# A mixture-of-experts layer in which the block for an expert's slots past 64 is split into an up half and a down half, with the ordinary up products between them

## The chip, the cores and the metric

The kernel runs on one core of a Trainium2 chip. The metric is device microseconds (us) of one execution; lower is better. Engines are named as the profile names them: PE is TensorE (PEld its weight loads), DVE is VectorE, ACT is ScalarE, POOL is GpSimd, SP is SyncE, which issues every DMA here. A name with a q behind it (PEldq, SPq) means the engine's sequencer.

## What is computed

One residual layer on 256 tokens of width 1024: a mixer (differential attention beside a gated linear recurrence), a layer norm, a top-4-of-32 mixture of experts with a clamped SwiGLU, and a second layer norm. The change lies in the mixture of experts alone:

```python
logits = xt @ w_router + b_router
top_v, top_e = lax.top_k(logits, 4);  gates = softmax(top_v)
# for each expert e and the tokens that chose it:
h = xb @ w_gu[e] + b_gu[e]                    # 1024 -> 2048, bias b_gu
x_glu = minimum(h[..., ::2], 7.0);  x_lin = clip(h[..., 1::2], -7.0, 7.0)
y = (x_glu * sigmoid(1.702 * x_glu) * (x_lin + 1.0)) @ w_down[e] + b_down[e]
out[token] += gate * y
```

All arithmetic is float32. The weights of the 32 experts are 403 MB, each read once.

## The kernel before

The first 125 us or so hold the mixer, the first norm and the router. The rest is a loop over the experts. Every expert has 64 fixed slots (CAP): a matmul with a one-hot matrix gathers its tokens' activations, 64 columns per expert. Tokens past the 64th of an expert go to overflow blocks of 32 slots (OCAP), which run under a branch on the expert's token count.

**Weights.** `load_chunk` loads an expert's weights in six chunks of 2 MB, four for the up product (w_gu, one DMA each) and two for the down product (w_down, two DMAs of 1 MB each), into ten slots that are used in turn. `ahead` issues, on SP's queue and in this order, the load that goes into a slot when the matmuls that read the slot have been issued; the DMA itself waits for those matmuls. At most eight DMAs are under way: the issue of one also waits for the landing of the one eight before it.

**One ordinary expert on PE** (PE and SP run in the order written; DVE, ACT and POOL are ordered by a planner within each stretch between branches):

1. `overflow(e)`: the branch L1011 on the count; in most cases its body is jumped over.
2. `first(e)`: 64 matmul passes of up products (`gu_mm`, L892). The bias is already in the accumulators (`begin_gu`, L679, fp32r). While these run, `ready(e + 1)` (L1002) loads the count of the next expert into registers of PE, DVE and ACT, and gives PE a prefetch hint for the branch. DVE and ACT do the SwiGLU (L902 to L906).
3. `finish`: the combine of the pair of experts before (L954, with adds on DVE, L956). Odd experts: the transposes of the gates (`gate_t`, L948, copied by ACT, L950).
4. `act_t`: transposes of the activations (L913), each followed by the next expert's bias (`begin_gu`).
5. `need`: the gather of a later pair's columns (L797), then the down products (L925), and the next expert.

The pool `mc` has three PSUM tiles that the combines, transposes, gathers and overflow blocks use in turn, so that a stage that takes a tile waits until the stage three tiles before has been read out.

**The overflow block before** (`more`), at the head of the expert's iteration: gather of 32 columns, bias (four f32 matmuls, L688), up products in four groups of 32 columns (L892), SwiGLU, transposes of activations and gates (L913, L981), down products (L988), copy (L991), eight small combines with eight adds on DVE (L996, L997). In this input one expert has more than 64 tokens, and no more than 96: the block runs once. It is expert 25, since six more experts follow it. Experts 30 and 31 share the last stretch, in which both up products come before the two down products.

## Time and profile before

| | |
|---|---|
| median of 3 runs | 1098.63 us (1097.76 to 1101.21) |
| profiled execution | 1100.57 us, of which the span of the trace is 1098.9 us |
| PE busy | 1008.3 us, 92% of the span |
| mean granted clock of PE | 0.979 of full speed |
| DMA | 423.4 MB, 385 GB/s over the span |

The profiled execution is one execution; 1.7 us of its time lie outside the span. Starts are in us from the span's start.

### The profile page before, as it was taken

How to read it: one execution, taken by the hardware profiler on the slowest of the kernel's cores; microseconds unless marked ns; L12 is line 12 of the kernel's file. 1: busy time of each engine (PE TensorE's matmuls, PEld its weight loads, DVE VectorE, ACT ScalarE, POOL GpSimd, SP SyncE). 2: the span in 40 equal slices, each digit the busy share in tenths (PEclk: the TensorE clock that was granted, in tenths of full speed). 3: DMA queues.
4: the chain of work that ended last, by engine and by line, in shares of the span. 5: the costliest groups of instructions: out<-in, count | busy, mean ns of one | idle time of the engine just before them, and what ended most of it. 6: DMA issues, size and time to landing. Idle time of an engine off the chain costs nothing. (4 is left out here: it accounts for less than half of the span.)

```text
span 1098.9 us, 12603 instructions
## 1 busy us (share of the span) xinstructions
PE 1008.3 (92%) x4948; PEld 472.8 (43%) x4948; DVE 277.8 (25%) x625; ACT 188.7 (17%) x426; POOL 146.6 (13%) x221
## 2 busy tenths in 40 slices
PE   8999999999999889888999989888888989999995
PEld 8987644443444333333334433333323434444431
DVE  6978411121212121213212121212101222121223
ACT  5576211111111111110011111110100101111111
POOL 4583202010101010101001010101001001010101
PEclk8999999999999999999899999999999989999998
DMA  7967799999999999999999999999999949999972
GB/s 268 334 247 318 293 377 426 422 423 423 423 423 423 422 423 423 422 425 426 423 424 420 410 423 412 420 410 394 415 395 411 423 198 424 425 425 422 424 292 82
DMA packets 47193, 423.44 MB, mean 385 GB/s; under 512 B 6365, under 2 KB 6430, under 8 KB 14400
## 3 DMA queue, kind: packets, MB, share of 16 engines
q1 hardware_dynamic: 47040, 421.59, 92.9%
q8 instruction: 73, 1.20, 0.5%
q14 instruction: 80, 0.66, 0.2%
HBM read 420.52 MB, written 1.05 MB: 384 GB/s over the span
## 5 line engine op out<-in xcount | busy, mean ns | idle before, releaser
L892 PE MATMUL h<-we,xg 128*64 128x512 f32 (+1 forms) x2112 | 469.8, 603 | 63.1 <-DMA we<-in_w_gu_dram 50.6
L892 PEld LDWEIGHTS h<-we,xg 128*64 128x64 f32 (+1 forms) x2112 | 161.9, 137 | 368.3 <-issue 295.1
L925 PE MATMUL y<-we,actT 128*64 128x512 f32 x1024 | 228.9, 599 | 0.1
L902 DVE TENSOR_SCALAR g<-h 128x256 f32<-128x256 f32 x65 | 27.6, 425 | 688.3 <-PE h L892 688.3
L940 POOL TENSOR_SCALAR sgate<-iota,posm,gate 128x64 f32<-128x64 f32 x96 | 54.1, 582 | 814.2 <-PE gt_ps L948 813.2
L925 PEld LDWEIGHTS y<-we,actT 128*64 128x64 f32 x1024 | 71.3, 137 | 135.1 <-issue 127.7
L903 ACT ACTIVATE sg<-g 128x256 f32<-128x256 f32 x65 | 27.0, 416 | 589.2 <-DVE g L902 589.2
L797 PE MATMUL xg_ps<-S,n 128*128 128x128 f32 (+1 forms) x544 | 70.5, 284 | 0.0
L797 PEld LDWEIGHTS xg_ps<-S,n 128*128 128x128 f32 x544 | 69.5, 199 | 2.5 <-issue 1.6
L954 PE MATMUL cb<-ysb,gtT 128*128 128x512 f32 x116 | 57.5, 618 | 0.0
L1117 ACT ACTIVATE ysb<-y 128x512 f32<-128x512 f32 x30 | 16.3, 594 | 140.7 <-PE y L925 140.7
L956 DVE TENSOR_TENSOR acc<-acc,cb 128x512 f32<-128x512 f32 x58 | 39.5, 680 | 0.0
L805 DVE TENSOR_SCALAR xg<-xg_ps,gb 128x128 f32<-128x128 f32 (+1 forms) x68 | 22.8, 398 | 61.8 <-PE xg_ps L797 61.8
L389 PE MATMUL pj<-xh,hi 128*128 128x256 f32 x128 | 37.3, 292 | 0.0
L389 PE MATMUL pj<-xh,lo 128*128 128x256 f32 x128 | 36.8, 288 | 0.0
L389 PE MATMUL pj<-xo,hi 128*128 128x256 f32 x128 | 36.8, 288 | 0.0
L913 PE MATMUL actT_ps<-ident,g 128*128 128x128 f32 x130 | 29.9, 312 | 7.3 <-DVE g L906 6.3
L954 PEld LDWEIGHTS cb<-ysb,gtT 128*128 128x128 f32 x116 | 19.6, 189 | 37.4 <-ACT sg L903 23.5
L252 POOL TENSOR_TENSOR lo<-win,hi 128x1024 fp32r<-128x1024 f32 x11 | 32.9, 3014 | 12.3 <-PE pj L389 12.2
L913 PEld LDWEIGHTS actT_ps<-ident,g 128*128 128x128 f32 x130 | 21.6, 202 | 24.8 <-DVE g L906 12.2
L807 ACT ACTIVATE xg<-xg_ps,gb 128x128 f32<-128x128 f32 (+1 forms) x68 | 25.4, 452 | 33.2 <-PE xg_ps L797 33.2
L679 PE MATMUL h<-bgu,pick 128*128 128x512 f32 x64 | 30.5, 479 | 0.0
(271 smaller groups left out, 702.5 us busy)
## 6 DMA issues: line engine op xcount, KB each, us to landing
we<-in_w_gu_dram SPq DMA_DIRECT2D x128, 2048.0 KB, 15.3
we<-in_w_down_dram SPq DMA_DIRECT2D x127, 1024.0 KB, 30.4
win<-in_w_in_dram SPq DMA_DIRECT2D x8, 1024.0 KB, 9.8
wout<-in_w_out_dram SPq DMA_DIRECT2D x4, 1024.0 KB
win<-in_w_in_dram SPq DMA_DIRECT2D x4, 512.0 KB, 8.2
x<-in_x_dram SPq DMA_DIRECT2D x4, 256.0 KB, 3.1
we<-in_w_down_dram SPq DMA_DIRECT2D x2, 512.0 KB
out_dram<-acc SPq DMA_DIRECT2D x4, 256.0 KB, 2.3
```

What stands on the lines that cost most here:

```text
L252: return (eng or V).tensor_sub(lo, src, f32(hi))
L389: PE.matmul(ps[m // 2][:, m % 2], a, b, start=k == 0 and m % 2 == 0 and i == 0, stop=k == KT - 1 and i == 2, skip_group_check=True)
L679: PE.matmul(ps[b], picks[e].rearrange("p g w -> p (g w)"), bgs[b], start=True, stop=False, skip_group_check=True)
L797: PE.matmul(ps[:, (k % 4) * n:(k % 4 + 1) * n], pairs(n1[t])[:, k // 2, k % 2], S[:, t], start=start, stop=t == NT - 1, skip_group_check=True)
L892: PE.matmul(ps[b][g * w:(g + 1) * w], xg[k // 4][:, k % 4, o:o + w], W[e, k][:, c0:c0 + 512], start=False, stop=k == KT - 1, skip_group_ch ...
L902: V.tensor_scalar(g[:, ns], ps[b][:, 0::2], 7.0, None, op0=OP.min)
L903: A.activation(s, g[:, ns], AF.Sigmoid, scale=1.702)
L913: PE.transpose(ps[:, j * P:(j + 1) * P], gj[:, j], ident)
L925: PE.matmul(ps[n][gs], at[:, 2 * b + j, g * CAP:(g + 1) * CAP], w_dn(e, 2 * g + b, j, n * 512, 512), start=c + j == 0, stop=c + j == 4, sk ...
L940: G.tensor_scalar(sg[:, t, i * CAP:(i + 1) * CAP], iota2[:, 0], posm[:, t, o:o + 1], gate[:, t, o:o + 1], op0=OP.is_equal, op1=OP.mult)
L954: PE.matmul(pp, gt[:, n, t * P:(t + 1) * P], y, start=True, stop=True)
L956: V.tensor_add(acc[t][:, ns], acc[t][:, ns], pp)
```

## The change

`more` becomes `more_up` (gather, bias, up products, gate transposes, SwiGLU) and `more_down` (activation transposes, down products, combines). For all experts but the last, `overflow(e)` runs `more_up` at the old place, ahead of the ordinary up products, and `overflow_down(e)` runs `more_down` under a second branch on the same count, behind `finish` and the gate transposes. The rarer blocks past 96 slots are now ahead of the first one within the branch. The load of the next expert's count and its hint (`ready(e + 1)`) move behind the second branch; their old place is taken by a hint for the second branch. The bias of the overflow block is made by two fp32r matmuls over all 128 columns, as that of the ordinary block, with a stationary matrix that DVE spreads out first. The gate matrix is built once and copied three times instead of built four times, and the eight combines go into four PSUM tiles, two to a tile.

```diff
     def begin_more(e):
         ps = mc(f"h{e}")
-        for q in range(4):
-            g, b = q // 2, q % 2
-            pick = two[:, 32 * g + e:32 * g + e + 1].to_broadcast([P, OCAP])
-            PE.matmul(ps[q * OCAP:(q + 1) * OCAP], pick, f32(bgs[b]), start=True, stop=False, skip_group_check=True)
+        pick = wk.tile([P, 2, P], F32R, tag="l", name=f"picko{e}")
+        V.memset(f32(pick), 0.0)
+        for b in range(2):
+            V.tensor_copy(pick[:, b].rearrange("p (g b c) -> p b g c", g=2, b=2)[:, b], picks[e][:, :, :OCAP])
+        for b in range(2):
+            PE.matmul(ps, pick[:, b], bgs[b], start=b == 0, stop=False, skip_group_check=True)
         return {0: ps}
...
-    def more(e, i):
+    def more_up(e, i):
         pm = shifted(e, i)
         xg = gather([e], OCAP, pm, V, "o")
+        sg = wk.tile([P, NT, P], F32, tag="sg", name=f"sgateo{e}")
         for half in range(2):
             gather_mm(*xg, half)
...
+        h = gu_mm(e, xg[1], 0, OCAP)
         for t in range(NT):
-            for g in range(ng):
-                V.tensor_scalar(sg[:, t, g * OCAP:(g + 1) * OCAP], iota2[:, 0, 0:OCAP], pm[:, t, 0:1],
-                                gate[:, t, e:e + 1], op0=OP.is_equal, op1=OP.mult)
+            V.tensor_scalar(sg[:, t, :OCAP], iota2[:, 0, 0:OCAP], pm[:, t, 0:1], gate[:, t, e:e + 1],
+                            op0=OP.is_equal, op1=OP.mult)
+            V.tensor_copy(sg[:, t, OCAP:].rearrange("p (g c) -> p g c", c=OCAP),
+                          sg[:, t, None, :OCAP].to_broadcast([P, P // OCAP - 1, OCAP]))
         ps = mc(f"gto_ps{e}")
         for t in range(NT):
             PE.transpose(ps[:, t * P:(t + 1) * P], sg[:, t], ident)
+        gt = wk.tile([P, T], F32, tag="gto", bufs=1, name=f"gtTo{e}")
         A.activation(gt, ps[:, :T], AF.Copy)
+        g = wk.tile([P, 256], F32, tag="go", bufs=1, name=f"go{e}")
+        swiglu(e, h, 0, g)
+        return g, gt
+
+    def more_down(e, g, gt):
+        ng, n = P // OCAP, 256
+        ao = wk.tile([P, 2, P], F32, tag="l", name=f"actTo{e}")
+        act_t(e, g, 0, ao)
         ps = mc(f"yo{e}")
...
-        for t in range(NT):
-            for g in range(ng):
...
+        for g in range(ng):
+            gs, ns = slice(g * OCAP, (g + 1) * OCAP), slice(g * n, (g + 1) * n)
+            pp = mc(f"cbo{e}_{g}").rearrange("p (t n) -> p t n", t=NT)
+            for t in range(NT):
+                PE.matmul(pp[:, t], gt[gs, t * P:(t + 1) * P], y[gs, :], start=True, stop=True, skip_group_check=True)
+            for t in range(NT):
+                V.tensor_add(acc[t][:, ns], acc[t][:, ns], pp[:, t])
+
+    def more(e, i):
+        more_down(e, *more_up(e, i))
...
+    def overflow_down(e):
+        with tc.If(counts[e] > CAP, preferred_fallthrough_block=True, label=f"down{e}"):
+            more_down(e, *held.pop(e))
...
     for e in range(NE - 1):
         if e > 0:
             overflow(e)
-        g = first(e, lambda i: (i == 3 and ready(e + 1), e == 0 and i == 6 and need(0, V, 1)))
+        g = first(e, lambda i: (i == 3 and hint(f"down{e}", counts[e] > CAP), e == 0 and i == 6 and need(0, V, 1)))
         finish(e % 2)
         if e % 2 == 0:
             sg = gate_rows(e)
         else:
             gt = gate_t(e, sg)
+        overflow_down(e)
+        ready(e + 1)
         at = wk.tile([P, 4, P], F32, tag="actT", bufs=1, name=f"actT{e}")
```

## Rows read from the trace of the kernel before

**Rows 1.** From the page: the span, and the DMA rate in 40 slices of 27.5 us.

```profile
span 1098.9 us, 12603 instructions
...
GB/s 268 334 247 318 293 377 426 422 423 423 423 423 423 422 423 423 422 425 426 423 424 420 410 423 412 420 410 394 415 395 411 423 198 424 425 425 422 424 292 82
```

**Rows 2.** Waits, all of the run, and PE's longest in total from 896 us on: who waited for whom, us in total, times, longest.

```profile
PE h L892 <- DMA we<-in_w_gu_dram: 50.6, 39, 2.4
```

```profile
PE h L892 <- PEq L1011: 0.9, 5, 0.2
```

**Rows 3.** Timeline of PE: the start of the ordinary up products of experts 22, 23, 26 and 29 (start, us, engine, line, operation, out<-in, shape, count, idle before and what ended it).

```profile
773.68 1.90 PE L892 MATMUL h<-we,xg 128*64 128x512 f32 x7 [0.19 <-PEq L1011]
...
804.67 3.65 PE L892 MATMUL h<-we,xg 128*64 128x512 f32 x16 [1.21 <-DMA we<-in_w_gu_dram]
...
925.07 2.37 PE L892 MATMUL h<-we,xg 128*64 128x512 f32 x10 [0.18 <-PEq L1011]
...
1003.65 13.95 PE L892 MATMUL h<-we,xg 128*64 128x512 f32 x64 [0.16 <-PEq L1011]
1017.53 1.98 PE L954 MATMUL cb<-ysb,gtT 128*128 128x512 f32 x4
```

**Rows 4.** Timeline of PE through expert 25: its overflow block, its ordinary up products, combine and gate transposes; and two rows of DVE and ACT in the same stretch.

```profile
869.71 1.94 PE L688 MATMUL h<-bgu,two 128*32 128x512 f32 x8
871.42 6.03 PE L892 MATMUL h<-we,xg 128*32 128x512 f32 x48
879.85 3.50 PE L892 MATMUL h<-we,xg 128*32 128x512 f32 x16 [2.40 <-DMA we<-in_w_gu_dram]
...
886.54 0.70 PE L913 MATMUL actT_ps<-ident,g 128*128 128x128 f32 x2 [3.19 <-DVE g L906]
887.03 0.63 PE L981 MATMUL gto_ps<-ident,sgateo 128*128 128x128 f32 x2
887.71 4.71 PE L988 MATMUL yo<-we,actTo 128*32 128x256 f32 x64
...
892.94 0.71 PE L996 MATMUL cbo<-yo,gtTo 32*128 32x256 f32 x6 [0.51 <-ACTq L1017]
893.67 3.17 DVE L997 TENSOR_TENSOR acc<-acc,cbo 128x256 f32<-128x256 f32 x8 [7.19 <-PE cbo L996]
...
896.83 15.58 PE L892 MATMUL h<-we,xg 128*64 128x512 f32 x64 [0.45 <-PEq L1017]
...
912.33 1.98 PE L954 MATMUL cb<-ysb,gtT 128*128 128x512 f32 x4
...
914.15 0.60 PE L948 MATMUL gt_ps<-ident,sgate 128*128 128x128 f32 x4
...
914.59 0.40 PE L913 MATMUL actT_ps<-ident,g 128*128 128x128 f32 x2
...
914.79 0.60 ACT L950 ACTIVATE gtT<-gt_ps 128x512 f32<-128x512 f32 x1 [1.40 <-PE gt_ps L948]
...
915.83 2.04 PE L797 MATMUL xg_ps<-S,n 128*128 128x128 f32 x16
```

**Rows 5.** Windows of 5 us: busy time of PE, PEld, DVE, ACT and POOL (with instructions), granted PE clock, DMA share, GB/s.

```profile
885.00:890.00 5.00, 3.42 (x28) 1.87 (x32) 1.48 (x6) 0.77 (x2) 0.00 (x0) 0.66 0.65 274
890.00:895.00 5.00, 3.99 (x59) 2.16 (x48) 1.21 (x4) 0.38 (x1) 0.00 (x0) 1.00 0.07 28
895.00:900.00 5.00, 4.55 (x15) 1.68 (x15) 1.72 (x5) 0.00 (x0) 0.00 (x0) 0.67 0.08 29
```

**Rows 6.** The branch and the count on PE's sequencer: line, engine, operation, count; min/median/max ns, first and last start. The first row is of the whole run, the second of 900 to 1030 us, the last two of 896 to 898 us.

```profile
L1011 PEldq COMPARE_BRANCH  x32: 82/783/4019, 125.5 to 1071.0; - x32
```

```profile
L1011 PEldq COMPARE_BRANCH  x5: 359/397/1197, 920.4 to 1025.6; - x5
```

```profile
L1002 PEldq TENSOR_LOAD <-cnt x1: 307/307/307, 896.9 to 896.9; - x1
```

```profile
L1219 PEldq BRANCH_PREFETCH_HINT  x1: 40/40/40, 897.7 to 897.7; - x1
```

**Rows 7.** The end. PE's up products of expert 31 and the down products that come last; what the SP queue waited for in 1050 to 1052 us; and two windows of 5 us (columns as in rows 5).

```profile
1047.34 8.80 PE L892 MATMUL h<-we,xg 128*64 128x512 f32 x40
...
1077.05 7.09 PE L925 MATMUL y<-we,actT 128*64 128x512 f32 x32
```

```profile
SPq L199 <- DMA we<-in_w_gu_dram: 4.6, 1, 4.6
```

```profile
1050.84 0.33 SPq L199 DMA_DIRECT2D we<-in_w_down_dram  x1
```

```profile
1065.00:1070.00 5.00, 4.53 (x21) 1.95 (x19) 0.42 (x1) 0.77 (x2) 0.00 (x0) 1.00 0.07 25
1070.00:1075.00 5.00, 5.00 (x18) 1.49 (x20) 0.00 (x0) 0.00 (x0) 0.00 (x0) 1.00 0.08 26
```

**Rows 8.** From the page: the DMA queues that carry instructions (packets, MB, share of 16 engines). From the timeline of PE: the activation transposes of expert 0.

```profile
q8 instruction: 73, 1.20, 0.5%
q14 instruction: 80, 0.66, 0.2%
```

```profile
144.30 0.50 PE L913 MATMUL actT_ps<-ident,g 128*128 128x128 f32 x2 [1.06 <-DVE g L906]
...
146.10 0.70 PE L913 MATMUL actT_ps<-ident,g 128*128 128x128 f32 x2 [1.07 <-DVE g L906]
```

More of the change, by code (lines that the diff above doesn't have):

```diff
@@ L981, in more @@
             PE.transpose(ps[:, t * P:(t + 1) * P], sg[:, t], ident)
-        gt = wk.tile([P, T], F32, tag="sg", name=f"gtTo{e}")
+        gt = wk.tile([P, T], F32, tag="gto", bufs=1, name=f"gtTo{e}")
         A.activation(gt, ps[:, :T], AF.Copy)
+        g = wk.tile([P, 256], F32, tag="go", bufs=1, name=f"go{e}")
[5 more added lines that the diff above has]
+        act_t(e, g, 0, ao)
         ps = mc(f"yo{e}")
@@ L991, in more @@
         A.activation(y, ps[:, :n], AF.Copy)
-        for t in range(NT):
-            for g in range(ng):
-                gs, ns = slice(g * OCAP, (g + 1) * OCAP), slice(g * n, (g + 1) * n)
-                pp = mc(f"cbo{e}_{t}_{g}")
-                PE.matmul(pp[:, :n], gt[gs, t * P:(t + 1) * P], y[gs, :], start=True, stop=True)
-                V.tensor_add(acc[t][:, ns], acc[t][:, ns], pp[:, :n])
+        for g in range(ng):
[7 more added lines that the diff above has]
+        more_down(e, *more_up(e, i))
     counts = {}
@@ L1008, in overflow @@
     def overflow(e):
-        c = counts.pop(e)
+        c = counts[e]
+        last = e == NE - 1
         with tc.If(c > CAP, preferred_fallthrough_block=True, label=f"over{e}"):
             hint(f"more{e}_1", c > CAP + OCAP)
-            if e == NE - 1:
+            if last:
                 for t in range(NT):
                     V.memset(acc[t], 0.0)
-            more(e, 0)
             with tc.If(c > CAP + OCAP, preferred_fallthrough_block=True, label=f"more{e}_1"):
@@ L1023, in overflow @@
                         more(e, i)
-            if e == NE - 1:
+            if last:
+                more(e, 0)
                 for t in range(NT):
                     fin(t, ident, acc[t])
+            else:
+                held[e] = more_up(e, 0)
+    held = {}
+    def overflow_down(e):
+        with tc.If(counts[e] > CAP, preferred_fallthrough_block=True, label=f"down{e}"):
+            more_down(e, *held.pop(e))
     where = {e: (i, j) for i, g in enumerate(GROUPS) for j, e in enumerate(g)}
```

6 lines of the change are left out of this document (removed).

## Prediction, made before the changed kernel was run

> **What bounds the kernel now.** I read the page's DMA rate first: from slice 7 on, but for the last two, it stands near 420 GB/s, with one hole, 198 GB/s in slice 33, where expert 25's overflow block lies [rows 1]. So the loop streams weights at a nearly constant rate, and PE is close behind. Which of the two sets the pace is read from PE's waits and from the distance of two experts. Ahead of 896 us PE waits for weights 39 times, 50.6 us in all; behind it the longest entry of its waits is a branch, 0.9 us, and there is none for weights [rows 2]. Experts 22 and 23 start 31.0 us apart; from expert 26 to 29 three experts take 78.6 us, 26.2 us each [rows 3]. The reader is to see two stretches: up to expert 25 the weights are the bound, with 4 to 5 us of slack on PE in every expert; the overflow block then puts PE behind by its whole length, the weights run ahead, and from there to the end PE is the bound.
>
> How far ahead are the weights at the end? A DMA issue waits for the landing of the one eight before. The issue at 1050.84 us had waited 4.6 us for a w_gu load [rows 7]; it is the seventh w_down issue behind the eight w_gu loads of experts 30 and 31, so what landed there is expert 31's third chunk. PE uses it from about 1054.2 us: it starts at 1047.34 and makes 16 passes per chunk, 64 of them in 13.88 us [rows 3, 7], so 1047.34 + 32 x 0.217 = 1054.3. The slack is 3.4 us. Nothing that makes PE faster ahead of this can gain more than 3.4 us, unless the weights land sooner.
>
> Would they? In the hole the rate is not zero but 28 GB/s, and again 25 and 26 GB/s in the last stretch, when all other loads are through [rows 5, 7]. That is 1/16 of 424 GB/s: one of the 16 DMA engines is behind the others and still works while they have nothing. A load has landed when its last part has. So the hole is time in which 15 engines wait for slots and the one that decides goes on. I take it that the last landings stay where they are.
>
> **The change, part by part.** All times are in the profiled execution.
>
> *Bias in fp32r.* The eight f32 passes take about 1.7 us up to the first up product (869.71 to 871.42) [rows 4]; two passes of 128 columns may take half of that. The last 16 up products of the block wait for a weight chunk for 2.40 us [rows 4]. What is saved ahead of 879.85 us makes that wait longer: nothing gained. By the same cover the pick matrix that DVE now builds costs nothing, and so does the branch to the rarer blocks, now at the head: DVE's and PE's time there lies inside the wait. Without that cover the bias would be worth 0.8 us.
>
> *The overflow block's stall.* From the end of its up products (879.85 + 3.50 = 883.35) to the ordinary ones (896.83) PE spends 13.5 us: 3.19 waiting for SwiGLU, transposes, 4.71 of down products, 0.51 for a copy, combines held up by DVE's adds, 0.45 for the branch [rows 4]. Afterwards only the two gate transposes remain there, 0.6 us; SwiGLU runs under the ordinary up products. Removed: 12.9 us.
>
> *The same work, now behind the gate transposes.* Added there: 0.4 for the transposes, 0.6 for ACT's copy of the ordinary gates that is ahead of theirs, and 0.3, an estimate, for what their own copy takes beyond that; then the down products, 3.8 us at full clock (4.71 with the first half at 0.66 [rows 4, 5]); 0.5 for the copy; 0.7 to the first add; eight adds in 3.17 us, because the next gather needs the last of the three PSUM tiles back [rows 4]. That is 9.5 us. Under the adds run the ordinary transposes and biases, 1.24 us (914.59 to 915.83 [rows 4]). Added: 8.3 us. Bounds: 6.5 if the combines and adds overlap better, 11 if every copy and add is waited for.
>
> *The clock.* The ordinary up products of expert 25 took 15.50 us (896.83 to 912.33) against 13.88 for expert 29: the granted clock was 0.67 in 895 to 900, after a stretch of waits [rows 3 to 5]. They now follow 16 passes without a pause, so I take the full rate, a gain of 1.6 us. But the thinly filled stretch has only moved, and the low clock may follow it there. I give back half, 0.8 us (bounds 0 and 1.6).
>
> Sum for expert 25: 12.9 - 8.3 + 1.6 - 0.8 = 5.4 us gained, between 1.9 and 8.0.
>
> *A second branch and a moved count, for every expert.* The load of the count and the hint take PE's sequencer 0.86 us (896.88 to 897.74 [rows 6]). At the old place the sequencer is ahead of PE by many passes, and the rows show no wait for it. The new place is behind the second branch. When a body is jumped over, PE first runs dry: in the rows the next work follows a branch with a gap of 0.16 to 0.19 us [rows 3]. Then the 0.86 us follow with PE empty. Less what PE waits for there anyway (the transposes need DVE's SwiGLU), some 0.3 us, I take 0.95 us per expert. Bounds: 0.2 if the sequencer is early enough for all of it, 1.7 if part of a slow branch shows. What is queued behind on PE is the transposes, the gather and the down products; ACT's and DVE's own branch and count lie under these.
>
> Up to expert 25 this is covered by the 4 to 5 us of slack. For the first experts, where SP still waits for PE, PE waits over 1 us for DVE at this very place (expert 0, twice [rows 8]), so the loads do not start later. From expert 26 to 30 there is no cover: 5 x 0.95 = 4.8 us lost, between 1.0 and 8.5.
>
> One rule speaks against this part. The rows: a jump took PE's sequencer 0.08 us at least, 0.78 at the median, 4.02 at most [rows 6], and was mostly hidden, because PE had passes left. The Trainium skill, page "Runtime: NRT & Kernel Launch", section "Instruction fetch mechanics", says that a taken branch whose target is outside the window already fetched stops until a DMA has brought the page. The longest rows agree; by the rule alone every new jump would be exposed, and the five experts would lose far more than 4.8 us. That is the first rival below.
>
> **The sum.** -5.4 + 4.8 = -0.6 us: 1098.3 for the span of 1098.9, 1099.9 for the profiled execution of 1100.57. That execution is 1.9 us above the median; for the median, 1098.63 - 0.6 = **1098.0 us**. What a measurement of this kernel can tell from no change is about 0.3%, 3.3 us.
>
> **The rivals.**
>
> *The new jump stalls PE (slower).* Each of the five late experts pays the time of a slow jump less what PE has queued. For it: jumps of up to 4.02 us [rows 6], with less work queued ahead of the new branch than ahead of the old. Against: most are short, and the hint is given some 14 us ahead. It decides from (5.4 + 3.3) / 5 = 1.75 us per expert; at 3 us it gives 1098.6 - 5.4 + 15 = 1108 us. Chance 0.12.
>
> *More code to fetch delays the weights (slower).* Instructions come by DMA too, 1.86 MB in 153 packets [rows 8], beside the engine that decides the landings. If every added branch puts 1 us in front of it, 25 experts with the weights as bound are 25 us later: about 1120 us. Against: the code is hardly longer, and a jump over a short body lands in what is fetched anyway. Chance 0.06.
>
> *The weights do land sooner (faster).* The hole is about 13 us long at full rate (27.5 us at 198 instead of 424 GB/s lose 14.6 us). The ordinary up products now free their slots some 13 us earlier. If the slots decide and not the one slow engine, the end can move by what PE gains, and PE would have to gain it: 8.0 at most for expert 25, less 1.0: 1098.6 - 7 = 1091.6 us. Against: the 25 to 28 GB/s. Chance 0.14.
>
> *The change does what I say*: 0.68. Its own range: gains end at the 3.4 us of slack, 1095.2; losses at -1.9 + 8.5, 1105.2.
>
> **How the numbers follow.** I predict 1098.0, the likeliest case. The range leaves out the second rival (0.06) and about as much again at each end of the first and the third: 1094.5 to 1107. Within 0.3% ends at 1095.3 and 1101.9. Of the 0.68, 0.58 lies inside, 0.08 above, 0.02 below. Faster: 0.02 + 0.14 = 0.16; slower: 0.08 + 0.12 + 0.06 = 0.26; same: 0.58.
>
> **What would show it.** In expert 25: no wait for DVE behind the last overflow up product, and ordinary up products of 13.9 us that begin near 884; the next expert's begin near 919.7 instead of 925.07. No hole in the rate below 300 GB/s for more than a few us. Experts 26 to 29 at 27 us each instead of 26.2, with a gap on PE ahead of the activation transposes. The last down products start within 3.4 us of 1077.05. I am wrong if the distance of experts 22 and 23 changes, since then the change reaches the stream of weights; if the late experts stay at 26.2 us; or if weights land at the end well ahead of 1075.

## The result and the profile after

The changed kernel is slower: 1112.64 us (median of four, 1110.47 to 1115.91) against 1099.77 us for the kernel before on the same chip; the ratio is 1.0123, interval 1.0103 to 1.0142. I had predicted 1098.0 us, and 1107 us as the upper end. In the profiled executions the span goes from 1098.9 to 1109.2 us, 10.3 us against 12.9 between the medians; the profiled execution of the changed kernel is 1.7 us under its median, that of the kernel before 0.8 us over it. What follows places the 10.3 us.

The page of the changed kernel, span, DMA rate in 40 slices and the two queues that carry instructions (compare [rows 1, 8]):

```profile
span 1109.2 us, 12977 instructions
...
GB/s 258 302 286 326 281 390 427 419 423 423 421 422 421 423 424 422 422 422 424 367 424 420 424 421 421 424 419 420 405 420 410 422 339 346 421 422 423 420 113 77
...
q8 instruction: 109, 1.79, 0.7%
q14 instruction: 86, 0.70, 0.2%
```

The hole of 198 GB/s has become two shallow ones, 339 and 346. Queue 8 went from 73 to 109 packets of 16 KB. It carries PE's code: the section on the hints shows PE's stalls ending just behind its packets.

The timeline of PE through expert 25 (compare [rows 4]):

```profile
870.72 4.46 PE L799 MATMUL xg_ps<-S,n 128*128 128x32 f32 x28 [2.85 <-DVE S L786]
875.99 1.06 PE L799 MATMUL xg_ps<-S,n 128*128 128x32 f32 x4 [0.81 <-issue]
876.86 1.20 PE L690 MATMUL h<-bgu,picko 128*128 128x512 f32 x2
877.99 7.86 PE L894 MATMUL h<-we,xg 128*32 128x512 f32 x64
885.79 0.44 PE L980 MATMUL gto_ps<-ident,sgateo 128*128 128x128 f32 x2
886.15 13.96 PE L894 MATMUL h<-we,xg 128*64 128x512 f32 x64
900.04 1.98 PE L956 MATMUL cb<-ysb,gtT 128*128 128x512 f32 x4
...
912.65 2.55 PE L799 MATMUL xg_ps<-S,n 128*128 128x128 f32 x16
...
922.40 1.08 PE L894 MATMUL h<-we,xg 128*64 128x512 f32 x4 [0.18 <-PEq L1024]
```

The stall between the two groups of up products is gone, and the ordinary ones run at the full rate. But the block starts late: its gather waits 2.85 us for DVE's selection rows (S) and 0.81 us for nothing that the profile names ("issue"), and there is no wait for weights left to hide that.

PE in expert 28, from the same timeline:

```profile
991.34 1.98 PE L956 MATMUL cb<-ysb,gtT 128*128 128x512 f32 x4
994.68 0.48 PE L915 MATMUL actT_ps<-ident,g 128*128 128x128 f32 x2 [1.36 <-DVEq L1046]
...
995.69 0.39 PE L799 MATMUL xg_ps<-S,n 128*128 128x128 f32 x2
1000.05 3.15 PE L799 MATMUL xg_ps<-S,n 128*128 128x128 f32 x14 [3.97 <-issue]
1003.12 8.46 PE L927 MATMUL y<-we,actT 128*64 128x512 f32 x32
```

Two new things: 1.36 us ahead of the activation transposes, which end with something of DVE's sequencer on L1046, the second branch; and a stall of 3.97 us in the middle of the gather, behind which gather and down products run 2.7 us longer than in other experts, since the granted clock was 0.50, its lower level, from 1000 to 1005 us, behind the stall. PE's waits over the whole run have both (us, times, longest):

```profile
PE actT_ps L915 <- DVEq L1046: 22.9, 17, 2.0
PE xg_ps L799 <- issue: 16.4, 5, 4.5
PE actT_ps L915 <- ACTq L1046: 16.0, 13, 1.4
...
PE y L927 <- issue: 6.7, 4, 3.0
```

**Where the time went.** Expert 24 starts at 836.9 instead of 836.0: +0.9. From there to expert 26 (922.40; before 925.07): 85.5 us instead of 89.1, -3.6. From expert 26 to 30 (1039.5): 117.1 us instead of 105.2, +11.9; three of the four intervals are 27.3, 27.8 and 27.7 us where 26.0 and 26.6 were usual, and the one with the stall 34.3. Behind that +1.1, one more gap of 1.19 us. Sum: 0.9 - 3.6 + 11.9 + 1.1 = 10.3 us, the difference of the spans.

### The profile page after: what moved, and what is told of

It is laid out like the page before. It is cut to its first block, busy times and chain, and to the rows that moved or that the text cites. A ratio compares the mean times of both kernels' runs of the same rounds, so it can differ in the third digit from the quotient of the medians.

```text
span 1109.2 us, 12977 instructions
## 1 busy us (share of the span) xinstructions
PE 1008.7 (91%) x4942; PEld 488.4 (44%) x4942; DVE 277.5 (25%) x624; ACT 194.6 (18%) x427; POOL 146.2 (13%) x221
## 5 line engine op out<-in xcount | busy, mean ns | idle before, releaser
L894 PE MATMUL h<-we,xg 128*64 128x512 f32 (+1 forms) x2112 | 457.3, 595 | 14.2 <-DMA we<-in_w_gu_dram 8.8
L894 PEld LDWEIGHTS h<-we,xg 128*64 128x64 f32 (+1 forms) x2112 | 170.7, 136 | 297.6 <-issue 277.9
L927 PE MATMUL y<-we,actT 128*64 128x512 f32 x1024 | 235.2, 609 | 6.8 <-issue 6.7
L904 DVE TENSOR_SCALAR g<-h 128x256 f32<-128x256 f32 x64 | 27.1, 424 | 665.2 <-PE h L894 665.2
L905 ACT ACTIVATE sg<-g 128x256 f32<-128x256 f32 x64 | 26.6, 416 | 514.0 <-DVE g L904 514.0
L799 PE MATMUL xg_ps<-S,n 128*128 128x128 f32 (+1 forms) x544 | 77.7, 300 | 19.2 <-issue 16.4
L799 PEld LDWEIGHTS xg_ps<-S,n 128*128 128x128 f32 x544 | 76.6, 215 | 22.8 <-issue 21.7
L389 PE MATMUL pj<-xo,hi 128*128 128x256 f32 x128 | 36.7, 286 | 0.0
L389 PE MATMUL pj<-xh,lo 128*128 128x256 f32 x128 | 36.7, 286 | 0.0
L916 ACT ACTIVATE actT<-actT_ps 128x256 f32<-128x256 f32 x64 | 24.5, 384 | 68.5 <-PE actT_ps L915 66.3
```

What stands on the lines that cost most here:

```text
L389: PE.matmul(ps[m // 2][:, m % 2], a, b, start=k == 0 and m % 2 == 0 and i == 0, stop=k == KT - 1 and i == 2, skip_group_check=True)
L799: PE.matmul(ps[:, (k % 4) * n:(k % 4 + 1) * n], pairs(n1[t])[:, k // 2, k % 2], S[:, t], start=start, stop=t == NT - 1, skip_group_check=True)
L894: PE.matmul(ps[b][g * w:(g + 1) * w], xg[k // 4][:, k % 4, o:o + w], W[e, k][:, c0:c0 + 512], start=False, stop=k == KT - 1, skip_group_ch ...
L904: V.tensor_scalar(g[:, ns], ps[b][:, 0::2], 7.0, None, op0=OP.min)
L905: A.activation(s, g[:, ns], AF.Sigmoid, scale=1.702)
L927: PE.matmul(ps[n][gs], at[:, 2 * b + j, g * CAP:(g + 1) * CAP], w_dn(e, 2 * g + b, j, n * 512, 512), start=c + j == 0, stop=c + j == 4, sk ...
```

## The experiments

Differences are between medians, kernel less the kernel before on the same chip; the changed kernel itself stands at +12.9. Runs of one kernel spread over some 5 us (one_branch: 1095.2 to 1101.0), so a profile's intervals tell where time goes, and the medians how much.

| kernel | median us | less before | ratio, interval |
|---|---|---|---|
| one_branch | 1098.29 | -0.7 | 1.0001, 0.9990 to 1.0012 |
| count_late | 1099.19 | +0.2 | 1.0008, 0.9996 to 1.0019 |
| count_back | 1107.51 | +8.5 | 1.0081, 1.0067 to 1.0094 |
| spare_branch | 1108.89 | +9.9 | 1.0089, 1.0076 to 1.0103 |
| branch_later | 1105.98 | +6.9 | 1.0060, 1.0045 to 1.0074 |
| spare_one_tile | 1108.39 | +9.3 | 1.0094, 1.0080 to 1.0109 |
| rare_last | 1099.53 | +0.5 | 1.0006, 0.9997 to 1.0014 |
| later_rare_last | 1100.30 | +1.2 | 1.0011, 0.9996 to 1.0027 |
| after_rare_last | 1106.72 | +7.9 | 1.0061, 1.0036 to 1.0085 |
| one_rare_last | 1099.07 | +0.2 | 0.9993, 0.9982 to 1.0004 |
| hint_mid | 1124.93 | +26.1 | 1.0234, 1.0208 to 1.0261 |
| later_hint_mid | 1135.57 | +36.7 | 1.0328, 1.0306 to 1.0350 |
| after_no_hint | 1102.04 | +2.7 | 1.0030, 1.0019 to 1.0042 |
| rare_last_no_hint | 1103.82 | +4.5 | 1.0049, 1.0036 to 1.0062 |
| rare_last_late_no_hint | 1106.02 | +7.0 | 1.0067, 1.0053 to 1.0081 |
| own_tiles | 1098.98 | -0.4 | 0.9997, 0.9986 to 1.0008 |
| own_tiles_no_hint | 1097.59 | -1.8 | 0.9987, 0.9978 to 0.9997 |
| bias_only | 1102.41 | +3.4 | 1.0032, 1.0020 to 1.0044 |

### Is it the second branch?

**one_branch**

```diff
-                held[e] = more_up(e, 0)
+                more_down(e, *more_up(e, 0))
-        g = first(e, lambda i: (i == 3 and hint(f"down{e}", counts[e] > CAP), e == 0 and i == 6 and need(0, V, 1)))
+        g = first(e, lambda i: (i == 3 and ready(e + 1), e == 0 and i == 6 and need(0, V, 1)))
-        overflow_down(e)
-        ready(e + 1)
```

> The changed kernel with one branch again: the block's down products stand right behind its up products, ahead of the ordinary ones, and the count is loaded at its old place, in the middle of the ordinary up products; the fp32r bias, the rarer blocks at the head, the gate transposes ahead of SwiGLU and the four-tile combines stay. Theory S (the second branch on PE's sequencer, with the late count, costs the time): the gap ahead of the activation transposes goes from 1.2-1.4 us back to what DVE's SwiGLU leaves, experts 26 to 30 are 26.2 us apart, the whole run is 12 us or more under the changed kernel, between 1096 and 1101 us. Rival B (the cost is in the block of expert 25 itself, its order, its adds or the slow jump at its head): at most 3 us better than the changed kernel, above 1108 us.

Measured: no difference from the kernel before. All that the change costs is gone with the second branch, its hint and the count that moved with it: theory S, as far as these three go together. What it gains is gone too by the median; in the profile, the fastest of its eleven runs, expert 24 to 26 still take 85.9 us instead of 89.1.

**count_back**

```diff
-        g = first(e, lambda i: (i == 3 and hint(f"down{e}", counts[e] > CAP), e == 0 and i == 6 and need(0, V, 1)))
+        g = first(e, lambda i: (i == 3 and (hint(f"down{e}", counts[e] > CAP), ready(e + 1)), e == 0 and i == 6 and need(0, V, 1)))
         overflow_down(e)
-        ready(e + 1)
```

> The changed kernel with only the load of the next expert's count and its hint back in the middle of the ordinary up products; both branches stay. Theory S1 (most of the loss per expert is the 0.86 us of load and hint behind the drained engine): the gap ahead of the activation transposes falls from 1.2-1.4 to 0.3-0.5 us, experts 26 to 30 gain 0.9 us each, 1108 us; the stalls of 1 to 4.5 us behind the jump stay. Rival S2 (the jump itself and the code behind it are the cost): less than 1.5 us better than the changed kernel.

**count_late** (the kernel before)

```diff
-        g = first(e, lambda i: (i == 3 and ready(e + 1), e == 0 and i == 6 and need(0, V, 1)))
+        g = first(e, lambda i: (e == 0 and i == 6 and need(0, V, 1)))
             gt = gate_t(e, sg)
+        ready(e + 1)
```

> The kernel before with only the load of the count and its hint moved behind the gate transposes; no second branch. Theory S1: 0.86 us per late expert less what DVE is waited for there, 5 x 0.5 to 5 x 0.86, 2.5 to 4.3 us slower than before. Rival S2 (without a branch ahead of it the sequencer runs ahead and hides the load): within 1 us of before.

**spare_branch** (the kernel before; its body never runs)

```diff
+    def spare_down(e):
+        with tc.If(held[e] > CAP + 3 * OCAP, preferred_fallthrough_block=True, label=f"down{e}"):
+            more_down(e, *(f32(bgs[i])[:, :256] for i in range(2)))
-        g = first(e, lambda i: (i == 3 and ready(e + 1), e == 0 and i == 6 and need(0, V, 1)))
+        g = first(e, lambda i: (i == 3 and (hint(f"down{e}", held[e] > CAP + 3 * OCAP), ready(e + 1)), e == 0 and i == 6 and need(0, V, 1)))
             gt = gate_t(e, sg)
+        spare_down(e)
```

> The kernel before with an added branch behind the gate transposes, hinted in the middle of the ordinary up products as in the changed kernel, around the same down part, on a condition that no expert meets; expert 25's block and the count stay as before. Theory S2 (the jump and the code behind it): a gap of 0.3-0.5 us ahead of the activation transposes in every expert, stalls of 1 to 4.5 us behind some of the jumps, one of them among experts 26 to 30: 5 to 9 us slower than before. Theory S1: 1.5 to 2.5 us slower. Rival B: within 1 us of before.

Measured: the late count by itself costs nothing (+0.2), since without a branch ahead of it the sequencer is early. The branch and its hint, without the late count, cost 9.9 us, the size of S2 and more, but not by its mechanism: there is no stall in the gather or the down products. Its late experts are 27.2 and 27.3 us apart instead of 26.0 and 26.6, 1.0 us more on average, or 5 us for five. The other 5 I can only place: expert 24 already starts at 840.9 instead of 836.0. Of these 4.9 us, 1.8 are there when expert 0 starts, ahead of any branch (128.9 us; the kernels lie between 125.0 and 128.9 there); why the rest comes is open. In count_back the same 27.2 and 27.3 stand: the late count is worth 0.3 to 0.5 us of the gap, not the 0.9 of S1, and yet count_back is 4.3 us better than the changed kernel. What it saved is eight of the nine stalls that the profile calls "issue", shown below to be waits for code. The ninth grew to 3.7 us; it lies in expert 25's own gather, and behind it the granted clock was 0.50 (875 to 885 us), so that expert 24 to 26 take 91.6 us here.

### What the branch itself costs

PE's waits in 925 to 1040 us in count_back:

```profile
PE actT_ps L915 <- DVEq L1046: 2.1, 2, 1.1
PE actT_ps L915 <- ACTq L1046: 1.5, 2, 0.7
```

What PE waits for on DVE's and ACT's sequencers is seen in one expert of count_back, in the rows of L1046 (line, engine, operation, count; ns, first and last start):

```profile
L1046 DVEq COMPARE_BRANCH  x1: 56/56/56, 970.4 to 970.4; - x1
L1046 ACTq COMPARE_BRANCH  x1: 45/45/45, 970.8 to 970.8; - x1
L1046 PEldq EVENT_SEMAPHORE  x1: 51/51/51, 970.8 to 970.8; - x1
L1046 DVEq EVENT_SEMAPHORE  x1: 21/21/21, 971.2 to 971.2; - x1
L1046 ACTq EVENT_SEMAPHORE  x1: 17/17/17, 971.4 to 971.4; - x1
```

and in the timelines of DVE, ACT and PE there:

```profile
970.50 0.68 DVE L958 TENSOR_TENSOR acc<-acc,cb 128x512 f32<-128x512 f32 x1
```

```profile
970.78 0.60 ACT L952 ACTIVATE gtT<-gt_ps 128x512 f32<-128x512 f32 x1 [1.41 <-PE gt_ps L950]
```

```profile
971.47 0.50 PE L915 MATMUL actT_ps<-ident,g 128*128 128x128 f32 x2 [0.73 <-ACTq L1046]
```

On DVE and ACT the jump takes 45 to 56 ns. But behind it each engine raises its semaphore by what the skipped body would have added, and does so only when its own work ahead of the branch is done: DVE behind the add that ends at 971.18, ACT behind the gate copy that ends at 971.38. PE starts at 971.47. Before, PE needed neither. In expert 29 its transposes start at 1019.79, while DVE's last add runs to 1020.38:

```profile
1019.79 0.40 PE L913 MATMUL actT_ps<-ident,g 128*128 128x128 f32 x2
```

```profile
1019.70 0.68 DVE L956 TENSOR_TENSOR acc<-acc,cb 128x512 f32<-128x512 f32 x1
```

It needs them now because six tiles of the body and the transposes' tile come in turn from the same three PSUM buffers; the buffer's last reader is, by the program, in the body. Three kernels take this theory (J) apart from the rival that the expectations from here on call S, the jump and the drain of PE's own sequencer.

**branch_later** (count_back)

```diff
-        overflow_down(e)
         at = wk.tile([P, 4, P], F32, tag="actT", bufs=1, name=f"actT{e}")
...
         need(where[e][0] + 1, G, where[e][1])
+        overflow_down(e)
```

> The kernel of count_back (changed kernel, count loaded in the middle of the up products) with the second branch moved on by one step: behind the activation transposes and the gather, ahead of the ordinary down products, which write no tile of the pool that the branch's body uses. Theory J (join: past the jump each engine adds to its semaphore what the body would have added, DVE and ACT only behind all they have queued ahead, and PE's next tile of the shared PSUM pool waits for these additions): the gap of 0.7 and 1.2 us goes, 0.2-0.3 us for the drained engine stays, experts 26 to 30 are 26.2-26.9 apart instead of 27.2-27.3, 3 to 4 us better than count_back: 1103.5 to 1104.5. Rival S (the jump and the drain of PE's own sequencer): the gap of about 1 us only moves to the down products, within 1.5 us of count_back's 1107.5.

**spare_one_tile** (spare_branch, the body's `mc` tiles all one tile)

```diff
-        act_t(e, g, 0, ao)
         ps = mc(f"yo{e}")
+        for j in range(2):
+            PE.transpose(ps[:, j * P:(j + 1) * P], gj[:, j], ident)
...
-            pp = mc(f"cbo{e}_{g}").rearrange("p (t n) -> p t n", t=NT)
+            pp = ps.rearrange("p (t n) -> p t n", t=NT)
```

> The kernel of spare_branch (before, with a branch that no expert takes behind the gate transposes) with a body of the same instructions that uses one tile of the shared PSUM pool instead of six, so that the next two tiles of the pool have no reader in the body. Theory J: the gap ahead of the activation transposes shrinks to 0.2-0.5 us and experts 26 to 30 are at most 26.9 apart; 3 us or more better than spare_branch's 1108.9. Rival S: the same gaps and the same time as spare_branch, 1107.5 to 1110.

**own_tiles** (rare_last, below)

```diff
-            more_down(e, *held.pop(e))
+            more_down(e, *held.pop(e), lambda n: pgu[-1].tile([P, 512], F32, tag="gu", name=n))
...
             act_t(e, g, b, at[:, 2 * b:2 * b + 2])
-            if e < NE - 2:
-                begin_gu(e + 1, (b,))
         need(where[e][0] + 1, G, where[e][1])
+        if e < NE - 2:
+            begin_gu(e + 1)
```

> The kernel of rare_last with the PSUM tiles of the second branch's body taken from the pool of the up products instead of the shared one, and the next expert's two bias products moved behind the gather, so that nothing PE does in the first 3 us behind the branch needs a tile that the body uses. Theory J: the gaps of 0.7 and 1.2 us go, experts 26 to 30 are 26.2 to 26.7 apart, 3 to 4.5 us better than rare_last, 1095 to 1096.5 (the weights' slack at the end allows 3.4 us against the kernel before). Rival S (PE's own drain and jump): within 1 us of rare_last's 1099.5.

Measured: in all three the waits for DVE's and ACT's sequencers shrink or go, as J says. PE's waits in 925 to 1040 us, first in spare_one_tile, then in branch_later, then in own_tiles:

```profile
PE actT_ps L913 <- DVEq L1052: 1.0, 2, 0.5
```

```profile
PE h L894 <- PEq L1024: 3.9, 3, 3.5
PE y L927 <- PEq L1046: 0.7, 2, 0.4
```

```profile
PE h L894 <- PEq L1024: 2.3, 4, 1.8
PE actT_ps L915 <- DVE g L908: 0.7, 2, 0.4
```

With one shared tile 1.0 us of the 3.6 is left (spare_branch has the same 3.6 as count_back); moved behind the gather or with tiles of its own, the branch leaves PE nothing of DVE's and ACT's sequencers to wait for. Undisturbed late experts are 26.2 and 27.1 (branch_later) or 26.7 and 26.9 us apart (own_tiles, where the two bias products moved too), instead of 27.2 and 27.3; in the kernel before it was 26.0 and 26.6. So J explains 0.5 to 0.6 of the 1.0 us per expert. The other 0.3 to 0.5 stay: in branch_later as waits of up to 0.4 us for PE's own sequencer, which is S in small, in own_tiles with waits of up to 0.4 us for DVE's SwiGLU, whose cause I did not follow. The times follow less well. own_tiles is 0.8 us better than rare_last, not 3 to 4.5; branch_later is 1.6 us better than count_back, not 3 to 4, because PE waited 3.5 us for its jump over the overflow block at one late expert, and the up products behind it 16.8 us (953.1 to 969.9) instead of 13.9; spare_one_tile is 0.6 us better than spare_branch, not 3, with a stall of 2.6 us for code in one of the late experts of its profile. What is saved at the join is in part lost again to code.

### The rarer blocks at the head

In the changed kernel, the branch over the rarer blocks, its whole run:

```profile
L1029 PEldq COMPARE_BRANCH  x1: 6127/6127/6127, 863.8 to 863.8; - x1
```

```profile
870.27 0.27 DVE L686 MEMSET picko<- 128x256 f32 x1 [11.47 <-PEq L1029]
870.46 0.26 DVE L786 TENSOR_SCALAR S<-iota,pm 128x32 f32<-128x32 f32 x2
```

DVE's selection rows, hence PE's gather, wait for its end, 870.0: the same join, here with PE as the last to come. The edit in all four kernels is this, in one_rare_last with the down part right behind (and with tiles of their own for the rarer blocks' gates, so that the held ones stay):

```diff
             hint(f"more{e}_1", c > CAP + OCAP)
+            held[e] = more_up(e, 0)
             with tc.If(c > CAP + OCAP, preferred_fallthrough_block=True, label=f"more{e}_1"):
...
-                held[e] = more_up(e, 0)
```

**rare_last** (count_back)

> The kernel of count_back with the branch to the rarer blocks back behind the first block (as in the kernel before), instead of at the head. Theory R (the jump over them took PE 6.1 us at the head of expert 25's block, and DVE's selection rows waited for it): no wait of PE for DVE ahead of the block's gather, its up products end 47 to 48 us behind the start of expert 24 instead of 53, the run 4 to 6 us better than count_back: 1101.5 to 1103.5. Rival W (hidden under the wait for weights, as I predicted): within 1 us of 1107.5.

**after_rare_last** (the changed kernel)

> The changed kernel, count late as it has it, with only the branch to the rarer blocks back behind the first block. Theory R (measured with the early count: 8 us): 5 to 8 us better than the changed kernel, 1105 to 1107.5, expert 26 starts 82 to 83 us behind expert 24 instead of 85.5. Rival W (here the weights or the code decide the start of the block): within 2 us of the changed kernel.

**one_rare_last** (one_branch)

> The kernel of one_branch (one block again, count early) with the rarer blocks' branch behind the first block. No second branch, so experts 26 to 30 stay 26.0 and 26.6 apart. Theory R: the block starts 4 us earlier and ends 2 to 4 us earlier, 1095 to 1097.5. Rival W: the weights set the end of the block's up products, 1098 to 1099.5.

**later_rare_last** (branch_later)

> branch_later and rare_last in one. If both theories hold the gains add, 8 to 9 us, up to the slack of the weights at the end (3.4 us against the kernel before): 1096 to 1099. If one falls: 1102 to 1104.

Measured: 8.0 us better than count_back, 5.0 than the changed kernel (against the kernel before on each chip), nothing (+0.9) where there is one branch, 5.7 better than branch_later. With the 8.0 us count_back's stall of 3.7 us in the block's gather is gone as well, which R had not counted. PE in rare_last:

```profile
867.95 3.96 PE L799 MATMUL xg_ps<-S,n 128*128 128x32 f32 x32
871.74 0.71 PE L690 MATMUL h<-bgu,picko 128*128 128x512 f32 x2
872.38 5.61 PE L894 MATMUL h<-we,xg 128*32 128x512 f32 x48
880.97 1.92 PE L894 MATMUL h<-we,xg 128*32 128x512 f32 x16 [2.98 <-DMA we<-in_w_gu_dram]
882.83 0.44 PE L980 MATMUL gto_ps<-ident,sgateo 128*128 128x128 f32 x2
883.71 13.95 PE L894 MATMUL h<-we,xg 128*64 128x512 f32 x64 [0.44 <-PEq L1032]
```

No wait for DVE; the weights again set the end of the block's up products (2.98 us), and expert 26 starts 81.5 us behind expert 24 (837.5 to 918.95), 7.6 us less than before. So the split does gain at expert 25, more than I forecast, and the five late experts take it back: 27.2 and 27.3 us apart. Theory R holds with two branches. With one it does not show: W, as I had it in the prediction.

rare_last and after_rare_last differ only in where the count and its hint stand, and lie at +0.5 and +7.9: with a second branch ahead of it the late count costs 7.4 us there. It brings the hint for the next expert's first branch from some 22 us ahead of that jump to some 6, and PE waits 18.5 us in all for that jump (L1024) instead of 4.7, in one late expert 2.9 us, behind a jump of 6.45 us. The change had this effect too, and I had not thought of it.

### The hints and the code behind the jumps

**hint_mid** (the changed kernel)

```diff
-        ready(e + 1)
+        count(e + 1)
...
             for j in range(4):
+                if j == 2:
+                    hint(f"over{e + 1}", counts[e + 1] > CAP)
                 down_mm(e, at, ps, j)
```

> The changed kernel with the count still loaded behind the second branch, but the hint for the next expert's branch given in the middle of the ordinary down products instead of right behind the jump. Theory H (a hint right behind a jump takes the fetch of the code that follows the jump, and PE then stalls in the gather or the down products): the nine stalls of 0.8 to 4.5 us there go down to two at most, no late interval over 28 us, 1105 to 1108. Rival P (the jump alone breaks the fetch, the hint is innocent): the stalls stay, 1111 to 1114.

**later_hint_mid** (later_rare_last, with the same lines in the down products)

> later_rare_last (second branch ahead of the ordinary down products, rarer blocks last) with the hint for the next expert's branch given in the middle of the down products instead of some 20 us earlier, ahead of the second jump. Theory H2 (the second jump makes PE lose the code that the early hint had fetched, hence jumps of 3.3 to 3.5 us at two of five late experts there): no late interval over 27.2 us, 1096 to 1098. Rival: the hint comes too late for its fetch and each jump over the block takes 1 us or more, 1101 to 1106.

Both theories fell. From one expert of hint_mid, the hint (L1246) and the jump that it was for (L1024):

```profile
L1246 PEldq BRANCH_PREFETCH_HINT  x1: 40/40/40, 960.2 to 960.2; - x1
```

```profile
L1024 PEldq COMPARE_BRANCH  x1: 3797/3797/3797, 962.8 to 962.8; - x1
```

The hint came 2.5 us ahead of the jump, and the jump ended at 966.6, 6.3 us behind the hint. The rival of later_hint_mid is what happened, in almost every expert: PE waited 63.2 us in all for that jump there, 15.8 us in later_rare_last; in hint_mid it was 13.3 us, 5.3 us in the changed kernel. And in hint_mid the stalls in gather and down products stayed (18.5 and 8.2 us): the hint behind the jump was not their cause.

**after_no_hint** (the changed kernel)

```diff
-        g = first(e, lambda i: (i == 3 and hint(f"down{e}", counts[e] > CAP), e == 0 and i == 6 and need(0, V, 1)))
+        g = first(e, lambda i: (e == 0 and i == 6 and need(0, V, 1)))
```

> The changed kernel without the hint for the second branch; nothing else. Theory D (that hint has its page fetched in the middle of the up products and pushes out code that PE needs soon, hence the stalls behind the jump and 109 fetched pages instead of 73): the stalls in the gather and the down products go, at most 90 pages, no late interval over 28 us, 5 us or more better than the changed kernel, 1104 to 1108. Rival U (unhinted, the jump itself waits for its target): the second branch takes 1 to 4 us in each expert, slower than the changed kernel, 1116 us or more.

**rare_last_no_hint** (rare_last, the same hint taken out)

> The kernel of rare_last (early count, rarer blocks last) without the hint for the second branch. Theory D: 80 pages or fewer instead of 92, the same intervals of 27.2 us, within 1.5 us of rare_last's 1099.5. Rival U: the five late experts pay 1 to 4 us each, 1104 us or more.

**rare_last_late_no_hint** (after_no_hint, rarer blocks last)

> after_no_hint with the rarer blocks last: what is left of the changed kernel with the late count when both suspected costs are taken away. If the two costs are independent: 6 us (after to after_rare_last) better than after_no_hint's 1102.0, cut off by the weights' slack at the end at 1097 to 1098.5. If both remove the same stalls for code: 1100.5 to 1102.5.

**own_tiles_no_hint** (own_tiles, the same hint taken out)

> own_tiles without the hint for the second branch. Theories J and D: as own_tiles, within 1 us, with fewer pages fetched. Rival U: 4 us or more slower than own_tiles.

Measured: without this one hint the changed kernel is 10.2 us better (+12.9 to +2.7; the profiled execution is the slowest of its seven runs, 5.0 us over their median). The stalls in gather and down products are gone, and no late interval is over 27.9 us. PE in after_no_hint, in the expert whose gather stalled above:

```profile
997.50 0.48 PE L915 MATMUL actT_ps<-ident,g 128*128 128x128 f32 x2 [1.19 <-DVEq L1046]
...
998.52 2.04 PE L799 MATMUL xg_ps<-S,n 128*128 128x128 f32 x16
```

The jumps are quick with the hint and without: 0.24 us at 987.8 and 0.34 us at 990.8. What differs is the next packet of queue 8. In after_no_hint it starts at 994.3, 3.2 us behind the jump's end. In the changed kernel the records of that queue have none between 978.6 and 997.6, and PE goes on at 1000.05. The queues of the changed kernel from 987.8 to 997.5 us, then a line of those from 997.5 to 999:

```profile
q1 hardware_dynamic: 475, 4.01, 98.8%
q14 instruction: 1, 0.01, 0.2%
```

```profile
q8 instruction: 1, 0.02, 4.5%
```

All nine stalls, of 0.8 to 4.5 us, end 1.2 to 1.5 us behind the end of a packet of queue 8, so they are waits for code. Over all experts of the changed kernel, the next packet starts 3.1 to 4.0 us behind the second jump's end in 23, and 9.0 to 9.9 us behind it in eight; these eight have eight of the nine stalls. (The ninth, and the remaining jump, are expert 25's, which runs the body.) A late packet alone makes no stall: in after_no_hint it starts 10.1 to 11.3 us behind eight of the jumps, but another one had started 0.3 to 4.7 us ahead of them. In the changed kernel the one before the eight late ones had started 10.5 to 14.5 us ahead of the jump. So D holds in that code comes too late behind these jumps when the hint is there, but not in its sign that less is fetched: 107 packets instead of 109. How the hint does it is not shown. Taking it out also moves all code behind it, and no run has something harmless of the same length in its place. Nor does it do it alone: with the hint and the early count, count_back has one such stall, and spare_branch, rare_last and own_tiles have none.

The Trainium skill ("Runtime: NRT & Kernel Launch", section "Instruction fetch mechanics") has a taken branch stop when its target is not in the window already fetched. By that, the jump itself should have cost the time; here the new jumps took at most 0.44 us, and the stall of expert 28 began 8 us behind the jump, in straight code behind the target.

But taking the hint out is no rule. In rare_last it costs 4.0 us: the jump over the rarer blocks then stalls (3.97 us ahead of expert 25's ordinary up products). In own_tiles taking it out gains 1.4 us. And rare_last_late_no_hint, which has both cures, is at +7.0 (1106.0 us), worse than both of its forecasts and than after_no_hint: its late intervals are the clean 27.3 and 27.8, and a stall of 3.58 us at expert 25 is back. The two costs are thus not independent. I take both to be places in a stream of code where PE meets a part not yet fetched; each edit moves the code and with it the places. Which edit meets which place I can't predict from these runs.

own_tiles_no_hint is the best version: 1097.59 us, ratio 0.9987, interval 0.9978 to 0.9997. By its interval that is a gain, but one under the 0.3% that one measurement can tell, and the best of eighteen kernels, so I do not count on it. Expert 26 starts 82.8 us behind expert 24 there, late experts are 26.7 and 26.9 apart, and between 925 and 1040 us PE waits for weights again, once, 1.1 us: the slack at the end is used up.

### The bias alone

**bias_only** (the kernel before)

```diff
-        for q in range(4):
...
-            PE.matmul(ps[q * OCAP:(q + 1) * OCAP], pick, f32(bgs[b]), start=True, stop=False, skip_group_check=True)
+        pick = wk.tile([P, 2, P], F32R, tag="l", name=f"picko{e}")
...
+            PE.matmul(ps, pick[:, b], bgs[b], start=b == 0, stop=False, skip_group_check=True)
```

> The kernel before with only the bias of the block in fp32r (two passes by a pick matrix that DVE builds, instead of eight f32 passes). My step: 0, the last up products of the block wait for weights anyway; within 1 us of before. Rival: DVE's building of the pick matrix is on the path, or the saved 0.7 us of PE counts: 0.5 to 2 us either way.

Measured: +3.4 us, and not where the bias is. PE in its expert 25, and PE's waits for weights over the whole run (before: 50.6, 39, 2.4 [rows 2]):

```profile
872.49 0.71 PE L690 MATMUL h<-bgu,picko 128*128 128x512 f32 x2
...
878.02 1.92 PE L894 MATMUL h<-we,xg 128*32 128x512 f32 x16 [1.25 <-DMA we<-in_w_gu_dram]
882.90 1.93 PE L894 MATMUL h<-we,xg 128*32 128x512 f32 x16 [2.96 <-DMA we<-in_w_gu_dram]
```

```profile
PE h L894 <- DMA we<-in_w_gu_dram: 65.3, 51, 3.0
```

The bias takes 0.71 us instead of 1.94, and the wait for weights behind it takes nearly all of that back, as predicted. But the weights are later already: expert 1 starts 1.7 us earlier than before and expert 24 1.9 us later (837.9). Queue 14, which I take to carry the code of the other engines, has 85 packets instead of 80, and the last landings slip by as much as that: between the 41st weight load and the last, 838.7 us instead of 833.8. That five more code packets delay the one DMA engine that decides the landings by 1 us each would fit, and is the second rival in small. It is argued, not shown: rare_last and own_tiles_no_hint have 84 packets and only 1.4 and 1.6 us of delay, the changed kernel 86 and none. More packets of queue 8 did no harm by themselves: count_late has 85 instead of 73 and stands at +0.2.

## Why the prediction was wrong, point by point

- **The overflow block's stall and the moved work: right.** The stall from the end of the block's up products to the ordinary ones went from 13.5 to 0.3 us, the gate transposes in it: 13.2 us removed (12.9 forecast). From the start of the ordinary combine, 900.04, to the gather at 912.65 are 12.6 us where 3.5 were: 9.1 added (8.3). The clock gave back 1.6 us on the ordinary up products, and the gather took 2.55 us instead of 2.04 (net 1.1, forecast 0.8). Together 5.2 us against a forecast of 5.4.
- **"The branch to the rarer blocks, now at the head, lies inside the wait": wrong.** The wait it was to lie in was 2.4 us and the jump 6.1. The block's up products ended 49.0 us behind expert 24's start instead of 47.3, so expert 25 gained 3.6 us and not 5.4; with the branch put back, 5 us of the whole run return. My own rows gave a jump up to 4.02 us [rows 6]; I had not set the one against the other.
- **"A second branch and a moved count", 0.95 us per expert: the size nearly right by luck, the mechanism in the main wrong.** (The terms that I named, a gap of 0.16 to 0.19 and 0.86 less 0.3, make 0.7 and not 0.95.) The regular intervals grew by 1.2 us, and 1.0 with the early count. Of this 1.0, PE's wait for DVE's adds and ACT's copy at the join is 0.5 to 0.6; what is left for the drained PE and other causes is 0.3 to 0.5, and the late load adds 0.3, not 0.86. I had written that "ACT's and DVE's own branch and count lie under" PE's work; I had looked at what is queued behind the branch, and not at what is queued ahead of it on the other engines and needed through the shared PSUM tiles.
- **The step that failed most: nothing for the code behind the jump.** From expert 26 on, 13.0 us were lost against 4.8 forecast: 6.0 in the regular growth, and 7.0 in one wait for code, 4.0 us long, with what ran slowly behind it at the low clock. The prediction has no term for it; its sum lets PE run on as soon as the jump and the load are through. My first rival has the sum (1.75 us per expert decide, 2.6 came; it gave 1108 us) and the wrong place: the jumps were short, what follows them was late. I gave it 0.12, because a hint "some 14 us ahead" seemed to speak against it. The hint came 10 to 11 us ahead in the late experts, and without it 10.2 of the 12.9 us are gone.
- **The weights.** The last landing stayed where it was (1077.2 us, before 1077.5), as forecast, so the third rival was wrong, and the second is wrong for the changed kernel as a whole, though in bias_only the last load lands 4.9 us later behind the 41st, and 3.1 us in spare_branch.
- **That up to expert 25 all is covered: right in the sum.** The intervals from expert 9 on, where the weights had mostly set the pace, became 27.3 to 34.4 us with stalls in every third (expert 13, with other work in it, aside), and expert 24 still started only 0.9 us later. But the slack is not 4 to 5 us in every expert: from expert 1 to 8 the kernel before runs at PE's pace, 25.8 to 26.6 us with one longer interval, and up to 400 us PE waits for weights three times. These experts did become slower (26.4 to 32.4 us); what they and the later ones lost came out of PE's waits for weights, 8.8 us in all instead of 50.6. My sign of being wrong, a changed distance of experts 22 and 23, came (32.8 us instead of 31.0), by a stall for code of 1.8 us and not by the weights.

Open is the rule by which an added hint or a moved block turns into a stall for code, whether the hint does it or the place to which it shifts the code, and why spare_branch is so late at expert 24.

## What to carry to other kernels

A branch that is jumped over was here a meeting of engines: behind it each raised its semaphore only when its own queue ahead was done, and PE, which then took a buffer that the body uses, waited for the last of them. So look at what is queued ahead of the branch on every engine, and give the body buffers that nobody needs soon after. Price a jump over a long body at its slowest row, unless a wait of that length covers it, and treat a hint as an edit with a price of its own: time the kernel with it and without it. When a count moves, its hint moves too: look how far ahead of its jump it then stands.

## What was not expected of the hardware

- In hint_mid, a hint that came 2.5 us ahead of its jump left a jump of 3.80 us; the jump was through 6.3 us behind the hint, and between 3.8 and 9.7 us in the other late experts.
- With a hint for a short jump (median 0.33 us with it and without) PE's code came late: at eight of the jumps, queue 8 started no packet between one 10.5 to 14.5 us ahead of the jump and one 9.0 to 9.9 us behind it, and PE stalled for up to 4.5 us. Without the hint none of these stalls was there.
- A stall for code cost twice: behind the 3.97 us of expert 28 the granted clock was 0.50 for 5 us, and gather and down products took 2.7 us longer.
- A load of a count into PE's registers with its hint, 0.86 us on the sequencer, made 0.2 us of difference to the run where no branch stood ahead of it (interval of the ratio 0.9996 to 1.0019).
